# The first mixer's beginning: its modulation as TensorE products, query and key products by channel tile

## The chip, the cores and the metric

The kernel runs on one core of a Trainium2 chip, as one launch. The metric is the device time of one execution in microseconds (us). Five engines work side by side, each with its own queue in program order: TensorE (PE; its weight loads PEld), VectorE (DVE), ScalarE (ACT), GpSimd (POOL) and SyncE (SP), which here issues the loads. They wait for each other by semaphores. Two levels of TensorE's clock appear in the profile, 1.2 and 2.4 GHz; the granted clock is written as a share of the upper one.

## The reference

A sequence of 256 tokens with 1024 channels passes through two blocks of two layers each. What the change touches is the beginning of the first layer of the first block:

```python
c_act = jax.nn.silu(c)
mod = (c_act @ w_ada[l] + b_ada[l])[:, None, :]
sh1, sc1, g1, sh2, sc2, g2 = jnp.split(mod, 6, axis=-1)
h = _rms(x, norm1[l]) * (1.0 + sc1) + sh1
y = _mlstm_mixer(h, a_w_in[j], a_b_if[j], a_h_norm[j], a_w_out[j])
x = x + g1 * y
```

`_mlstm_mixer` projects h to queries and keys (512 columns each), values, output gate (1024 each) and 8 gate columns, mixes the tokens with a gated, chunked recurrence (here as one masked product per head), normalises, multiplies by the sigmoid of the output gate and projects back. A layer of 16 experts follows.

## The kernel before

Activations lie with channels on partitions: 8 channel tiles (KT) of 128 x 256 tokens. A matrix product in 32-bit precision is made of three products: `split` writes a rounded copy of an operand, the high half (ACT, line 371 for weights), and the rest, the low half (DVE, line 374), and `mm3` (lines 381 to 383) forms high x high, high x low and low x high into one sum.

The modulation (`ada`, line 604) has 6 x 8 = 48 columns of 128 channels. For one column a weight tile of 128 x 1024 (512 KB) is multiplied by the condition, which has been copied to all partitions, and summed along each row: on DVE in one instruction (line 623), or, from column 16 on and for every other column, on POOL (line 620) with the sum on ACT (line 621). `first_block` (line 1787) has the columns in a list, `filler`, two at a time. The first 16 (shift and scale of the first norm) are made before anything else by `fill(8)`; the other 32 are taken out of the list as fills between pieces of the mixer: one after every second tile of the query/key products, one in each step of the value products, one after every second tile of the output gate and of the projection.

`pre1` then forms the norm: the squares of x are summed over channels with a constant matrix of ones (`x_squares`, line 466 on PE), `rstd` makes the reciprocal root on DVE (lines 412 to 422), `row` spreads it over the partitions (PE, line 427), and `pre` scales each channel tile (DVE, line 475) and splits it into the halves of u (ACT line 361, DVE line 362).

`mlstm` starts with a chain for the gates (16 products at line 1176, exponential and logarithm on ACT, running maxima on DVE at lines 1211 to 1216, decay tiles at 1231 to 1234). The query and key products (line 1238, `ws_tiles`) go tile by tile of the output: 8 outputs, each over all 8 channel tiles with weights of one 512 KB load, evacuated by ACT (line 1239). The value products (`tokens_by_cols`) go over the channel tiles, two in a step, with four sums in PSUM. Then come the scores (line 1251), the mix, the output gate and the projection.

All loads are issued by SP in program order. Weights of the first mixer pass through a ring of 9 raw slots; a load waits until the slot's last reader is done. The order on each engine comes from a scheduler of the framework, which places the instructions when the program is built. Behind the mixer the same queue issues the expert weights.

The second mixer (`ada_first`, lines 634 to 664) already has 16 modulation columns of another matrix as TensorE products: the condition's 8 channel tiles stand as weights of 32 columns, the weight tile moves, the 8 products of a column fall on four groups of 32 partitions (line 661), a copy brings the 128 x 128 result into SBUF (line 663), and a product with a constant matrix of ones and zeros adds the four groups and turns the row into a column (line 653).

Of the kernel before, what the change touches and what calls it, by code (L numbers as in the profile page):

```python
# [19 lines left out]
KT = 8  # L20
# [141 lines left out]
def lay_out(inp):  # L162
# [17 lines left out]
    v.add("conds", np.stack([vec_cols(g["c_2"][0]), vec_cols(g["c_ctx_2"])], axis=2))  # L180
# [54 lines left out]
class Kernel:  # L235
# [16 lines left out]
    def load_first(self, pool):  # L252
# [4 lines left out]
        nc.sync.dma_start(self.xT, A["xT"])  # L257

    def load_second(self, pool):
        nc, A = self.nc, self.A  # L260
        nc.sync.dma_start(self.consts, A["consts"])
# [208 lines left out]
    def pre(self, pool, u, s, rb, gs, sh):  # L470

        nc = self.nc
        for k in range(KT):
            t = pool.tile([128, S], F32, tag="xs", name="xs", bufs=self.xs_bufs)
            nc.vector.scalar_tensor_tensor(t, self.xs(k, s), gs[:, k:k + 1], rb[:, :S], op0=ALU.mult, op1=ALU.mult)
            self.split_sum(u[:, k, 0], u[:, k, 1], t, sh[:, k:k + 1])
# [157 lines left out]

    def ada_first(self, pool):
# [3 lines left out]
        conds = pool.tile([128, KT, 32], F32, name="cond_cols", bufs=1)  # L639
        nc.gpsimd.memset(conds, 0.0)  # L640
        nc.scalar.activation(conds[:, :, :2], self.v("conds").rearrange("p (k s) -> p k s", s=2), AF.Silu)
# [7 lines left out]
        def some():  # L649
            if last:  # L650
                t, rows = last.pop()
                st = self.st()[:, :2]
                nc.tensor.matmul(st, rows, self.k("sum4")[:, :2], start=True, stop=True)
                nc.vector.tensor_add(self.mod2[0][:, t], st, self.v("b_ada2_0")[:, t:t + 1].to_broadcast([128, 2]))
            if todo:
                ps = self.tp()[:, :128]
                w = ahead.pop(0)
                ahead.extend(islice(raws, 1))
                for k in range(KT):
                    j = 32 * (k % 4)  # L660
                    nc.tensor.matmul(ps[j:j + 32], conds[:, k], w[:, k * 128:k * 128 + 128], start=(k < 4), stop=(k >= 4))
                rows = pool.tile([128, 128], F32, tag="grow", name="grow", bufs=2)
                nc.any.tensor_copy(rows, ps)
                last.append((todo.pop(0), rows))
# [411 lines left out]

    def router(self, wg, mod, g):
# [42 lines left out]
    def tokens_by_cols(self, u, src):  # L1120
# [43 lines left out]
    def mlstm(self, pool, u, gate, router):  # L1164
# [700 lines left out]
```

## Time and profile before

| | us |
|---|---|
| median of 3 runs | 2707.77 (2702.83 to 2710.92) |
| the profiled execution's own time | 2702.24 |
| its span in the profile | 2700.4 |
| first mixer: first weight product on DVE | 9.43 |
| first product of queries and keys on PE | 39.19 |
| last evacuation of queries and keys | 77.81 |
| copies of the values | 98.68 |
| first issue of expert weights into the ring | 152.68 |

A row of the timeline gives start, length, engine, line, what is written and read, shapes, and how many instructions it merges; in brackets the idle time before it and what ended it. A group by line gives busy time, mean of one in ns, and idle time before it. A stretch gives the busy time of every engine in it (with the number of instructions), the granted clock of TensorE, the share of the DMA engines and their rate.

### The profile page before, as it was taken

How to read it: one execution, taken by the hardware profiler on the slowest of the kernel's cores; microseconds unless marked ns; L12 is line 12 of the kernel's file. 1: busy time of each engine (PE TensorE's matmuls, PEld its weight loads, DVE VectorE, ACT ScalarE, POOL GpSimd, SP SyncE). 2: the span in 40 equal slices, each digit the busy share in tenths (PEclk: the TensorE clock that was granted, in tenths of full speed). 3: DMA queues.
4: the chain of work that ended last, by engine and by line, in shares of the span. 5: the costliest groups of instructions: out<-in, count | busy, mean ns of one | idle time of the engine just before them, and what ended most of it. 6: DMA issues, size and time to landing. Idle time of an engine off the chain costs nothing.

```text
span 2700.4 us, 38571 instructions
## 1 busy us (share of the span) xinstructions
PE 2476.7 (92%) x14614; PEld 1915.4 (71%) x14614; DVE 1653.1 (61%) x3421; ACT 935.7 (35%) x1641; POOL 473.4 (18%) x420
## 2 busy tenths in 40 slices
PE   3988997887999899999899999999899999898998
PEld 3874344566444688888775788888788888786997
DVE  7873125786222368656866777673858665958555
ACT  3541103564011232223327542222432223445543
POOL 2330101544000000002406420000400001534100
PEclk9989998888999899999899999999999999999999
DMA  8789997667999356532340236453247443322453
GB/s 320 276 327 410 420 419 261 232 211 298 381 398 419 141 185 221 168 120 88 135 138 1 79 110 209 154 190 91 74 148 226 155 150 97 118 83 94 160 178 123
DMA packets 123305, 540.62 MB, mean 200 GB/s; under 512 B 14688, under 2 KB 14944, under 8 KB 98272
## 3 DMA queue, kind: packets, MB, share of 16 engines
q1 hardware_dynamic: 123104, 538.00, 55.2%
q8 instruction: 119, 1.95, 0.3%
q14 instruction: 82, 0.67, 0.1%
HBM read 536.90 MB, written 1.05 MB: 199 GB/s over the span
## 4 chain that ended last, share of the span: by engine, by line
PE 56%; DVE 7%; issue 1%; ACT 1%; DMA 1%; POOL 0%; DVEq 0%; SPq 0%; ACTq 0%; POOLq 0%
PE mm L382 16%; PE mm L383 16%; PE mm L381 16%; DVE lo L374 2%; PE tp L383 1%; PE tp L382 1%; PE tp L381 1%; PE mm L868 1%; PE tp L860 1%; PE mm L848 1%; DVE ysq L499 1%; DMA raw<-in_w_ada_dram 1%; ACT hi L371 0%; DVE mx L818 0%; DVE rs_x L412 0%
## 5 line engine op out<-in xcount | busy, mean ns | idle before, releaser
L374 DVE TENSOR_TENSOR lo<-raw,hi 128x512 fp32r<-128x512 f32 (+1 forms) x780 | 574.7, 766 | 381.5 <-ACT hi L371 379.1
L371 ACT ACTIVATE hi<-raw 128x1024 fp32r<-128x1024 f32 (+1 forms) x390 | 404.7, 1044 | 872.3 <-PE mm L382 571.4
L381 PE MATMUL mm<-u,hi 128*128 128x512 f32 (+1 forms) x1608 | 572.8, 360 | 17.5 <-ACT hi L371 9.6
L383 PE MATMUL mm<-u,lo 128*128 128x512 f32 (+1 forms) x1608 | 576.8, 360 | 5.2 <-DVE lo L374 5.2
L382 PE MATMUL mm<-u,hi 128*128 128x512 f32 (+1 forms) x1608 | 578.2, 360 | 2.3 <-POOL u L359 1.3
L381 PEld LDWEIGHTS mm<-u,hi 128*128 128x128 f32 x1608 | 306.9, 193 | 64.5 <-ACT hi L371 11.2
L383 PEld LDWEIGHTS mm<-u,lo 128*128 128x128 f32 x1608 | 310.5, 193 | 49.1 <-DVE lo L374 6.9
L382 PEld LDWEIGHTS mm<-u,hi 128*128 128x128 f32 x1608 | 310.6, 193 | 47.3 <-DVE u L362 2.5
L382 PE MATMUL mm<-act,hi 128*128 128x512 f32 (+1 forms) x612 | 223.0, 364 | 0.1
L381 PE MATMUL mm<-act,hi 128*128 128x512 f32 (+1 forms) x612 | 222.3, 363 | 0.0
L383 PE MATMUL mm<-act,lo 128*128 128x512 f32 (+1 forms) x612 | 222.2, 363 | 0.0
L1691 PE MATMUL mm<-raw,xg 128*32 128x512 f32 x1696 | 199.2, 593 | 1.1 <-DMA raw<-in_moe_gu_dram 1.1
L623 DVE SCALAR_TENSOR_TENSOR junk<-raw,conds 128x1024 f32<-128x1024 f32 x128 | 155.6, 1222 | 66.3 <-DMA raw<-in_w_ada_dram 65.9
L620 POOL TENSOR_TENSOR raw<-raw,cond 128x1024 f32<-128x1024 f32 x48 | 119.9, 2502 | 244.7 <-DMA raw<-in_w_ada_dram 224.8
L501 POOL TENSOR_TENSOR acc<-acc,ysq 128x768 f32<-128x768 f32 x45 | 92.5, 2065 | 394.0 <-DVE ysq L499 348.8
L623 DVE SCALAR_TENSOR_TENSOR raw<-raw,conds 128x1024 f32<-128x1024 f32 x128 | 156.6, 1229 | 2.4
L628 POOL TENSOR_TENSOR mod<-mod,vecs 128x16 f32<-128x16 f32 (+1 forms) x28 | 10.3, 366 | 764.7 <-DVE raw L623 721.4
L1691 PEld LDWEIGHTS mm<-raw,xg 128*32 128x32 f32 x1696 | 63.0, 110 | 112.3 <-issue 107.6
L381 PEld LDWEIGHTS mm<-act,hi 128*128 128x128 f32 x612 | 117.5, 192 | 18.7 <-issue 1.2
L382 PEld LDWEIGHTS mm<-act,hi 128*128 128x128 f32 x612 | 117.7, 192 | 18.2 <-DVE act L351 0.7
L383 PEld LDWEIGHTS mm<-act,lo 128*128 128x128 f32 x612 | 117.5, 192 | 17.2
L1723 DVE TENSOR_TENSOR hy<-hy,tp 128x512 f32<-128x512 f32 x56 | 38.2, 686 | 149.3 <-PE tp L1720 149.1
(458 smaller groups left out, 4102.5 us busy)
## 6 DMA issues: line engine op xcount, KB each, us to landing
raw<-in_moe_gu_dram SPq DMA_DIRECT2D x122, 1024.0 KB, 17.8
raw<-in_w_ada_dram SPq DMA_DIRECT2D x200, 512.0 KB, 4.5
raw<-in_ffn_wi_dram SPq DMA_DIRECT2D x176, 512.0 KB, 4.3
raw<-in_moe_down_dram SPq DMA_DIRECT2D x63, 1024.0 KB, 17.8
raw<-in_ffn_wo_dram SPq DMA_DIRECT2D x48, 448.0 KB, 3.9
raw<-in_w_k_dram SPq DMA_DIRECT2D x32, 512.0 KB, 3.9
raw<-in_ffn_wo_dram SPq DMA_DIRECT2D x24, 512.0 KB, 4.2
raw<-in_ffn_wo_last_dram SPq DMA_DIRECT2D x22, 512.0 KB, 4.1
```

Source lines behind the costliest of these rows:

```text
L371: self.mark = self.nc.scalar.activation(hi[:, :m], raw[:, c:c + m], AF.Copy)
L374: self.nc.vector.tensor_sub(lo[:, i:e], raw[:, c + i:c + e], hi[:, i:e])
L381: nc.tensor.matmul(out, lh, rh, start=start, stop=False, skip_group_check=mixed)
L382: nc.tensor.matmul(out, lh, rl, start=False, stop=False, skip_group_check=mixed)
L383: nc.tensor.matmul(out, ll, rh, start=False, stop=stop, skip_group_check=mixed)
L499: nc.vector.scalar_tensor_tensor(t[:, 2], y, self.gate(d, s), kern.xs(d, s), op0=ALU.mult, op1=ALU.mult)
L501: (nc.vector if d == KT - 2 else nc.gpsimd).tensor_add(self.acc[s], self.acc[s], t)
L620: nc.gpsimd.tensor_mul(out, rows, c)
L623: nc.vector.scalar_tensor_tensor(out, rows, 1.0, c, op0=ALU.mult, op1=ALU.mult, accum_out=mod[:, t, s:s + 1])
L848: nc.tensor.matmul(sc[:, :nk], qk[a][half, 512 + t * 128:640 + t * 128], qk[b][half, :nk], start=(i == 0), stop=(i == 2))
L1691: nc.tensor.matmul(ps[t:t + 32], x[:, t:t + 32], w[i][:, s], start=first, stop=last)
L1723: nc.vector.tensor_add(yv, yv, tp)
```

## The change

The 16 columns of the first modulation are made by TensorE as in the second mixer, two per channel tile (shift and scale of that tile), from a new layout of the weights, `w_ada_first`. `first_input` goes over the channel tiles: it makes the columns of the next tile, forms the tile's u, and adds its share to all 8 query/key outputs, which are kept as sums in the four PSUM banks until the end; `a_qk` is laid out by channel tile for it. The outputs are evacuated by ACT and DVE in turn at the start of `mlstm`. The constants are loaded ahead of the condition, the second part of the constants and the gate weights behind all 24 tiles. The fills that stood among the query/key products move into the value products: two per step in place of one. The helpers `cond_cols`, `column` and `column_end` are split out of `ada_first`; the constant they sum with, `sum2`, now lies in the first load.

```diff
-    v.add("conds", np.stack([vec_cols(g["c_2"][0]), vec_cols(g["c_ctx_2"])], axis=2))
+    v.add("conds", np.stack([vec_cols(g["c"][0]), vec_cols(g["c_2"][0]), vec_cols(g["c_ctx_2"])], axis=2))
+    v.add("sum2", (np.arange(128)[:, None] % 32 == np.arange(2)[None, :]).astype(np.float32))
...
+    order = np.arange(2 * KT).reshape(2, KT).T.ravel()
+    A["w_ada_first"] = np.ascontiguousarray(still_tiles(g["w_ada"][0, :, :2048])[order])
...
-    A["a_qk"] = still_tiles(aw[:, :1024])
+    A["a_qk"] = np.ascontiguousarray(ktiles(aw[:, :1024]))
...
         nc.sync.dma_start(self.xT, A["xT"])
+        nc.sync.dma_start(self.consts, A["consts"])
...
+    def column(self, pool, conds, w):
+        nc = self.nc
+        ps = self.tp()[:, :128]
+        for k in range(KT):
+            j = 32 * (k % 4)
+            nc.tensor.matmul(ps[j:j + 32], conds[:, k], w[:, k * 128:k * 128 + 128], start=(k < 4), stop=(k >= 4))
+        rows = pool.tile([128, 128], F32, tag="grow", name="grow", bufs=2)
+        nc.any.tensor_copy(rows, ps)
+        return rows
+
+    def column_end(self, rows, out, bias):
+        nc = self.nc
+        n = out.shape[1]
+        st = self.st()[:, :n]
+        nc.tensor.matmul(st, rows, self.v("sum2")[:, :n], start=True, stop=True)
+        nc.vector.tensor_add(out, st, bias.to_broadcast([128, n]) if n > 1 else bias)
...
+    def first_input(self, pool, p, mod, g):
...
+        banks = [self.mm() for _ in range(4)]
+        out = [banks[m // 2][:, m % 2 * S:m % 2 * S + S] for m in range(8)]
...
+        def columns(k):
+            rows = [(t, self.column(p, conds, self.ring.raw(A["w_ada_first"][2 * k + i:2 * k + i + 1].rearrange("t p k -> p t k"))))
+                    for i, t in enumerate((k, KT + k))]
+            for t, r in rows:
+                self.column_end(r, mod[:, t], bias[:, t:t + 1])
+            nc.vector.scalar_tensor_tensor(gs[:, k:k + 1], mod[:, KT + k], 1.0, g[:, k:k + 1], op0=ALU.add, op1=ALU.mult)
+            return self.chunks(self.ring, A["a_qk"][k:k + 1].rearrange("k p n -> p k n"))
+
+        w = columns(0)
+        rb = p.tile([128, S], F32, name="rb_first", bufs=1)
+        nc.scalar.activation(rb, self.x_rows(pool), AF.Copy)
+        for k in range(KT):
+            self.pre_tile(pool, u, 0, rb, gs, mod[:, :KT, 0], k)
+            now = w
+            if k < KT - 1:
+                w = columns(k + 1)
+            for m in range(8):
+                self.mm3(out[m], *now[m], u[:, k, 0], u[:, k, 1], k == 0 and m % 2 == 0, k == KT - 1, True)
+        return u, out
...
-    def tokens_by_cols(self, u, src):
+    def tokens_by_cols(self, u, src, fills):
...
-            self.fill()
+            self.fill(fills)
...
-    def mlstm(self, pool, u, gate, router):
+    def mlstm(self, pool, u, q_and_k, gate, router):
...
+        qk = t_([128, 8, S], "qk")
+        for m, ps in enumerate(q_and_k):
+            scale = 1.0 if m < 4 else 128.0 ** -0.5
+            if m % 2:
+                nc.vector.tensor_scalar(qk[:, m], ps, scale, None, op0=ALU.mult)
+            else:
+                nc.scalar.activation(qk[:, m], ps, AF.Copy, scale=scale)
...
-        for m, ps in self.ws_tiles(self.ring, A["a_qk"], u, [S] * 8):
-            nc.scalar.activation(qk[:, m], ps[:, :S], AF.Copy, scale=(1.0 if m < 4 else 128.0 ** -0.5))
-            if m % 2:
-                self.fill()
-        acc = self.tokens_by_cols(u, A["a_v"])
+        acc = self.tokens_by_cols(u, A["a_v"], 2)
...
-                    self.filler = ada[0]
-                    self.fill(8)
+                    self.filler = ada[0][8:]
+                    u, q_and_k = self.first_input(pool, p, mod, self.v("norm1_0"))
                     self.load_second(pool)
```

The queue of SP from the second load on, before, up to the first query/key weights:

```order
L257 DMA xT<-in_xT_dram 128x2048
L600 DMA cond_75<-in_conds_dram 128x1024
L326 DMA raw<-in_w_ada_dram 128x1024 x16
L261 DMA consts<-in_consts_dram 128x1154
L262 DMA consts_72<-in_consts_dram 128x1054
L264 DMA rows<-in_rows_dram 128x312
L267 DMA wr<-in_w_router_dram 128x8x16
L1170 DMA g_224<-in_a_g_dram 128x64
L326 DMA raw<-in_a_qk_dram 128x1024 x2
```

and in the changed kernel:

```order
L260 DMA xT<-in_xT_dram 128x2048
L261 DMA consts<-in_consts_dram 128x1154
L605 DMA cond_76<-in_conds_dram 128x1024
L329 DMA raw<-in_w_ada_first_dram 128x1024 x2
L329 DMA raw<-in_a_qk_dram 128x1024
L329 DMA raw<-in_w_ada_first_dram 128x1024 x2
L329 DMA raw<-in_a_qk_dram 128x1024
L329 DMA raw<-in_w_ada_first_dram 128x1024 x2
```

The constants have moved ahead of the first weights; of every three weight tiles two are now of the modulation and one of queries and keys.

TensorE in the middle of the query/key products, before (`a` and `lf` belong to the gate chain):

```order
L381 MATMUL mm<-u,hi 128x256
L382 MATMUL mm<-u,hi 128x256
L383 MATMUL mm<-u,lo 128x256
L381 MATMUL mm<-u,hi 128x256
L382 MATMUL mm<-u,hi 128x256
L427 MATMUL tp<-consts,a 128x128 x8
L383 MATMUL mm<-u,lo 128x256
L381 MATMUL mm<-u,hi 128x256
L382 MATMUL mm<-u,hi 128x256
```

and in the changed kernel, from the first products of the fourth channel tile on (line 384 to 386 is `mm3`, 654 a column of the next tile, 664 its sum):

```order
L384 MATMUL mm<-u,hi 128x256 x2
L664 MATMUL st<-vecs,grow 128x1
L385 MATMUL mm<-u,hi 128x256
L386 MATMUL mm<-u,lo 128x256
L384 MATMUL mm<-u,hi 128x256
L385 MATMUL mm<-u,hi 128x256
L654 MATMUL tp<-raw,cond_cols 32x128 x8
L386 MATMUL mm<-u,lo 128x256
L385 MATMUL mm<-u,hi 128x256
L386 MATMUL mm<-u,lo 128x256
L384 MATMUL mm<-u,hi 128x256
L664 MATMUL st<-vecs,grow 128x1
```

Columns and sums of the next channel tile now stand between the products; the gate chain is no longer there.

VectorE in the last steps of the value products and the beginning of the scores, before (623 is a fill, `lo` a low half of value weights, `v` the copy of the values):

```order
L623 SCALAR_TENSOR_TENSOR raw,mod_0_78<-raw,cond_75 128x1024
L374 TENSOR_TENSOR lo<-raw,hi 128x512 x4
L623 SCALAR_TENSOR_TENSOR raw,mod_0_78<-raw,cond_75 128x1024
L374 TENSOR_TENSOR lo<-raw,hi 128x512 x4
L623 SCALAR_TENSOR_TENSOR raw,mod_0_78<-raw,cond_75 128x1024
L1245 COPY v<-mm 128x512 x2
L374 TENSOR_TENSOR lo<-raw,hi 128x512
```

and in the changed kernel (628 is a fill, 1307 the decay times the scores):

```order
L628 SCALAR_TENSOR_TENSOR raw,mod_0_79<-raw,cond_76 128x1024 x2
L377 TENSOR_TENSOR lo<-raw,hi 128x512 x4
L628 SCALAR_TENSOR_TENSOR raw,mod_0_79<-raw,cond_76 128x1024 x2
L377 TENSOR_TENSOR lo<-raw,hi 128x512 x4
L1300 COPY v<-mm 128x512
L628 SCALAR_TENSOR_TENSOR raw,mod_0_79<-raw,cond_76 128x1024
L1307 TENSOR_TENSOR dt_784<-dt_784,mm 128x256
L1307 TENSOR_TENSOR dt_785<-dt_785,mm 128x128
L1307 TENSOR_TENSOR dt_784<-dt_784,mm 128x256
L628 SCALAR_TENSOR_TENSOR raw,mod_0_79<-raw,cond_76 128x1024
```

Each step now has two fills on VectorE, and two more stand behind the copy of the values, one of them among the scores.

## Rows read from the trace of the kernel before

**Rows 1.** The page, part 1: busy time of each engine, share, instructions.

```profile
PE 2476.7 (92%) x14614; PEld 1915.4 (71%) x14614; DVE 1653.1 (61%) x3421; ACT 935.7 (35%) x1641; POOL 473.4 (18%) x420
```

**Rows 2.** Stretches: length, busy of PE, PEld, DVE, ACT, POOL, PEclk, DMA share, GB/s.

```profile
20.00:30.00 10.00, 0.00 (x0) 0.00 (x0) 9.80 (x18) 0.00 (x0) 1.22 (x2) 1.00 1.03 410
...
60.00:70.00 10.00, 10.00 (x83) 10.00 (x82) 8.58 (x32) 5.80 (x10) 1.27 (x1) 0.94 0.68 253
...
90.00:100.00 10.00, 10.00 (x45) 8.00 (x44) 8.80 (x12) 4.01 (x6) 4.84 (x3) 1.00 0.97 367
...
250.00:300.00 50.00, 43.84 (x315) 23.06 (x313) 16.74 (x32) 8.57 (x16) 9.63 (x5) 0.93 1.02 421
```

**Rows 3.** Timeline of SP, the issue of loads, 152 to 202 us.

```profile
152.68 15.39 SPq L326 DMA_DIRECT2D raw<-in_moe_gu_dram  x8
...
200.38 20.51 SPq L326 DMA_DIRECT2D raw<-in_moe_gu_dram  x12
```

**Rows 4.** Timeline of the beginning: start, length, engine, line, idle before, releaser.

```profile
9.43 1.23 DVE L623 SCALAR_TENSOR_TENSOR raw<-raw,cond 128x1024 f32<-128x1024 f32 x1 [9.43 <-ACT sq L459]
...
28.59 1.22 DVE L623 SCALAR_TENSOR_TENSOR raw<-raw,cond 128x1024 f32<-128x1024 f32 x1
...
30.05 3.54 PE L466 MATMUL st<-consts,sq 128*128 128x1 f32 x16 [30.05 <-DMA consts<-in_consts_dram]
...
35.43 0.69 PE L427 MATMUL tp<-consts,rs_y 128*128 128x128 f32 x2 [1.83 <-DVE rs_y L422]
...
39.19 0.58 PE L381 MATMUL mm<-u,hi 128*128 128x256 f32 x1 [3.07 <-ACT hi L371]
...
44.77 3.33 PE L1176 MATMUL st<-u,gw 128*16 128x256 f32 x16 [1.42 <-DVE gw L351]
...
47.93 0.28 PE L383 MATMUL mm<-u,lo 128*128 128x256 f32 x1
```

**Rows 5.** Second mixer: two timeline rows, then groups of instructions by line.

```profile
451.74 1.08 PE L661 MATMUL tp<-raw,cond_cols 128*32 128x128 f32 x16
...
496.41 1.08 PE L661 MATMUL tp<-raw,cond_cols 128*32 128x128 f32 x32
...
L653 PE MATMUL st<-consts,grow 128*128 128x2 f32 x30 | 4.9, 239 | 4.0 <-DVE grow L663 2.1 <-DVE mod L654 1.9
...
L663 ACT COPY grow<-tp 128x128 f32<-128x128 f32 x5 | 1.2, 260 | 5.0 <-PE tp L661 5.0
```

**Rows 6.** Groups by line, first 170 us: busy, mean ns, idle before, releasers.

```profile
L475 DVE SCALAR_TENSOR_TENSOR xs<-xT,gs,tp 128x256 f32<-128x256 f32 x8 | 3.4, 471 | 0.8 <-PE tp L427 0.8
...
L361 ACT ACTIVATE u<-xs,mod 128x256 fp32r<-128x256 f32 x8 | 3.6, 498 | 25.6 <-DVE xs L475 25.5
...
L620 POOL TENSOR_TENSOR raw<-raw,cond 128x1024 f32<-128x1024 f32 x16 | 40.8, 2547 | 53.2 <-DMA raw<-in_w_ada_dram 36.1 <-ACT hi L371 7.2 <-DVE lo L374 6.3
```

**Rows 7.** Timeline of ACT and DVE, then two groups of the first 170 us.

```profile
77.81 0.36 ACT L1239 ACTIVATE qk<-mm 128x256 f32<-128x256 f32 x1
...
82.35 2.49 DVE L374 TENSOR_TENSOR lo<-raw,hi 128x512 fp32r<-128x512 f32 x4
...
98.68 1.39 DVE L1245 COPY v<-mm 128x512 f32<-128x512 f32 x2 [1.19 <-PE mm L1134]
...
L374 DVE TENSOR_TENSOR lo<-raw,hi 128x512 fp32r<-128x512 f32 x64 | 54.4, 887 | 2.3 <-ACT hi L371 2.3
L623 DVE SCALAR_TENSOR_TENSOR raw<-raw,cond 128x1024 f32<-128x1024 f32 x32 | 42.4, 1350 | 9.4 <-ACT sq L459 9.4
```

**Rows 8.** Timeline of the gate chain: DVE and one ACT row.

```profile
51.61 1.28 ACT L1186 ACT_TABLE_LOAD   x1
...
59.70 0.42 DVE L1211 TENSOR_TENSOR am<-tp,consts 128x256 f32<-128x256 f32 x1 [0.94 <-PE tp L427]
...
67.42 0.42 DVE L1231 TENSOR_TENSOR dt<-tp,consts 128x256 f32<-128x256 f32 x1 [0.73 <-PE tp L427]
```

**Rows 9.** Stretch 57.9 to 61.3 us, columns as in rows 2.

```profile
57.90:61.30 3.40, 3.40 (x18) 3.40 (x17) 2.43 (x10) 0.91 (x1) 2.36 (x1) 0.50 0.84 318
```

More of the change, by code (lines that the diff above doesn't have):

```diff
@@ L257, in load_first @@
         nc.sync.dma_start(self.xT, A["xT"])
+        nc.sync.dma_start(self.consts, A["consts"])
     def load_second(self, pool):
         nc, A = self.nc, self.A
-        nc.sync.dma_start(self.consts, A["consts"])
         nc.sync.dma_start(self.consts1, A["consts1"])
@@ L470, in pre, with pre_tile @@
     def pre(self, pool, u, s, rb, gs, sh):
-        nc = self.nc
         for k in range(KT):
-            t = pool.tile([128, S], F32, tag="xs", name="xs", bufs=self.xs_bufs)
-            nc.vector.scalar_tensor_tensor(t, self.xs(k, s), gs[:, k:k + 1], rb[:, :S], op0=ALU.mult, op1=ALU.mult)
-            self.split_sum(u[:, k, 0], u[:, k, 1], t, sh[:, k:k + 1])
+            self.pre_tile(pool, u, s, rb, gs, sh, k)
+    def pre_tile(self, pool, u, s, rb, gs, sh, k):
+        t = pool.tile([128, S], F32, tag="xs", name="xs", bufs=self.xs_bufs)
+        self.nc.vector.scalar_tensor_tensor(t, self.xs(k, s), gs[:, k:k + 1], rb[:, :S], op0=ALU.mult, op1=ALU.mult)
+        self.split_sum(u[:, k, 0], u[:, k, 1], t, sh[:, k:k + 1])
     class Output:
@@ L651, in some @@
                 t, rows = last.pop()
-                st = self.st()[:, :2]
-                nc.tensor.matmul(st, rows, self.k("sum4")[:, :2], start=True, stop=True)
-                nc.vector.tensor_add(self.mod2[0][:, t], st, self.v("b_ada2_0")[:, t:t + 1].to_broadcast([128, 2]))
+                self.column_end(rows, self.mod2[0][:, t], self.v("b_ada2_0")[:, t:t + 1])
             if todo:
-                ps = self.tp()[:, :128]
                 w = ahead.pop(0)
                 ahead.extend(islice(raws, 1))
[L659 to L664, printed above, removed]
+                last.append((todo.pop(0), self.column(pool, conds, w)))
         self.next_first = some
@@ L1075, in pre1 @@
         return u
+    def first_input(self, pool, p, mod, g):
+        nc, A = self.nc, self.A
+        conds = self.cond_cols(p, 0, 1)
+        gs = p.tile([128, KT], F32, name="gs_first", bufs=1)
+        u = pool.tile([128, KT, 2, S], F32R, tag="u", name="u", bufs=1)
+        banks = [self.mm() for _ in range(4)]
+        out = [banks[m // 2][:, m % 2 * S:m % 2 * S + S] for m in range(8)]
+        bias = self.v("b_ada_0")
+        def columns(k):
[16 more added lines that the diff above has]
+        return u, out
     def router(self, wg, mod, g):
@@ L1811, in first_block @@
                     self.ada_first(p)
-                u = self.pre1(pool, mod, self.v(f"norm1_{l}"))
+                    u = self.pre1(pool, mod, self.v(f"norm1_{l}"))
                 router = lambda: self.router(wg, mod, self.v(f"norm2_{l}"))
                 if l == 0:
-                    self.mlstm(p, u, mod[:, 16:24], router)
+                    self.mlstm(p, u, q_and_k, mod[:, 16:24], router)
                     self.fill(len(self.filler))
```

11 lines of the change are left out of this document (7 added, 4 removed).

## The prediction

> **What bounds the kernel now.** I read the page first, then the stretches of the first 300 us, the timeline of the first mixer engine by engine, and last the prices of single operations, some of which the first mixer does not have yet and the second one does. The page names TensorE: busy 92% of the span [rows 1]. The stretches show that this is no single limit [rows 2]. From 20 to 30 us TensorE does nothing, VectorE is busy 9.80 of 10 us, the DMA engines are full (1.03). From 60 to 70 and from 90 to 100 us TensorE is full, and VectorE has 8.58 and 8.80 of 10. From 250 us, in the experts, the DMA engines set the pace (1.02, 421 GB/s). So this change is worth what it does to the end of the first mixer. From there the time passes on one for one: the queue starts on expert weights at 152.7 us behind the mixer's last tiles, and the next group is issued at 200.4 us, when the first experts free their slots [rows 3]. Both move with the mixer.
>
> The timeline of the beginning shows why TensorE is late [rows 4]. VectorE multiplies 16 weight tiles by the condition, from 9.43 to 29.8 us. The sums of squares wait until 30.05 us for a constant loaded behind those tiles. The row statistics end at 35.4 us. The first products start at 39.19 us, but halt until 47.9 us, because VectorE still owes the low halves. From there TensorE is nearly dense to the value copies at 98.68 us. What the reader is to see: VectorE's 19 us are at the front, and TensorE's real start is 47.9.
>
> **The change, part by part.** All sums are made against the profiled execution, 2702.24 us (span 2700.4 and 1.84 around it). The median of the three runs is 5.5 us above it.
>
> *First loads.* The constants go ahead of the condition. At the 410 GB/s of this stretch [rows 2] their 128 x 1154 fp32 numbers (591 kB) cost 1.45 us, so the first weight tile, in use at 9.43 us before [rows 4], is there at about 10.5.
>
> *Columns on TensorE.* 16 products of 1.22 us leave VectorE (19.5 us) [rows 4]. The second mixer shows the price on TensorE [rows 5]: one column is 16 records in 1.08 us at the half clock, two are 32 records in 1.08 us at full clock, the drain of the last included, so 0.4 us each. Each also needs a copy (0.26 us on ScalarE) and a summing product (two records of 0.24 us). These are the very operations, so no bound is needed.
>
> *Start-up.* In order on TensorE: column, copy, sum, column, copy, sum (4 us, to 14.5), sums of squares 3.54 us (to 18), statistics on VectorE 1.8 us (TensorE's wait for them) plus the two low halves that the order puts among them, 1.2 us (to 21), broadcast 0.69, its copy 0.4, scaling 0.47, high half 0.50 [rows 4, 6]: the first query/key product starts at about 24 us. Those 24 products begin at the half clock: the 16 gate products at 44.77 us took 3.33 us, 0.208 each, 256 columns at 1.2 GHz, after waits of 1.5 to 3 us; later 83 records fill 10 us [rows 2, 4], 0.117 each. I take 4.5 us, so 28.5.
>
> *Seven further channel tiles.* Each is 24 products (2.8 us), two columns (0.8), two sums (0.5): 4.1 us of TensorE. The order puts each sum a few products behind its column, and the column's drain (its last record lasts some 0.3 of the 1.08 us), the copy (0.26) and two hand-overs, 0.8 us by my estimate, are longer than those products (0.5 us): I add 0.3 per column, so 4.7. The floor is 4.1; the DMA engines would need 3 x 512 KB, 3.8 us, and do not bind. The other end is the chain from the last sum of a tile to the next tile's first product, two additions and the gain (0.2 each), scaling 0.47, high half 0.50, hand-overs 0.3, against 1.4 us of products left to cover it: 5.2. So 28.5 + 7 x 4.7 = 61.4, and 0.6 for fill multiplications on GpSimd that now run in here: 62 us (57 to 67). Before, the last query/key tile was evacuated at 77.81 us [rows 7]. This stage gains 16 us.
>
> *What has moved behind it.* Before, the gate chain and four fills ran beside the query/key products; now they stand behind, and the four steps of the value products carry two fills each. VectorE's list from 62 us to the value copies: 16 low halves (2.49 us per four [rows 7]) 10.0; six fills x 1.22 = 7.3, the other two standing behind the first copy; the gate chain: reductions 59.70 to 63.37 = 3.7, decay tiles 67.42 to 70.4 = 3.0, some 14 small ops of 0.16 = 2.2, and a wait of 2 us for ScalarE's two table loads of 1.28 us with an exponential between them [rows 8], 10.9 in all; four evacuations of 0.42, 1.7. Then GpSimd. Undisturbed, a low half takes 0.62 us and a fill 1.22; over the whole mixer their means are 0.887 and 1.350 [rows 7]. The excess, 64 x 0.265 + 32 x 0.13 = 21 us, I lay on GpSimd's 16 multiplications of 2.55 us [rows 6], during which an operation of VectorE can stand still: 1.3 each on these two lines, 1.65 with the others that are hit; none if the coincidence is by chance, 2.55 if every one blocks. Five fall into this stretch: 5 x 1.65 = 8.2 (0 to 12.7). Sum 38.1, and 0.9 for the last products: the copies start at 101 us against 98.68: +2.3 us. TensorE alone needs less: 96 products at 45 per 10 us [rows 2] are 21.3 us, gates 5.
>
> *Scores.* Two fills now stand among the score products, 2.4 us of VectorE; one falls into a wait, I take 1.5.
>
> *Everything else.* Output gate and projection keep their fills and order. Loads total the same. The second mixer's column code only reads another constant: nothing. Evacuations on two engines: counted.
>
> Sum: -15.8 at the query/key stage, +19.6 given back by what had been hidden beside it: **+3.8 us**, 2706 on the profiled execution, **2712 on the median**. I expect that the gain of the first 50 us is spent by 105 us.
>
> **The rivals.** *One, faster: TensorE sets the pace of the value stage.* If the first multiplications of GpSimd fall into the query/key stage and the gate chain's waits swallow low halves, VectorE's 38 us shrink to TensorE's 21.3 + 5 + 1.7 = 28. With a stage of 57 to 60 us the copies come at 86 to 88: -11 and 1.5 back, about -10 to -12; 2697. For it: VectorE will have slack of about 1.5 us in each channel tile. Against it: before, with half the fills in this stage, VectorE was already busy 8.80 of 10 us [rows 2].
>
> *Two, slower: TensorE stays at the half clock in the channel-tile loop.* A column, a wait for its copy, a few products, a wait for the row: from 57.9 to 61.3 us the granted clock was 0.50, 1.2 GHz [rows 9], after TensorE had waited in the gate chain. At 1.2 GHz a tile costs 24 x 0.208 + 2 x 0.8 + 0.5 + 0.6 = 7.7 instead of 4.7. Seven tiles are +21, with some of it hidden under fills: 2727 to 2732; it decides from three tiles on (9 us). Against it: no wait in the loop should reach 1 us, and the full stretches of before, with gaps that short, ran at 0.94 to 1.00 [rows 2]. The Trainium skill (TensorE: Matmul & The Clock Gate, HAM oscillation) speaks against this loop shape: with channel tiles outermost and a wait between short bursts, the clock drops at every tile, and it advises to do all channel tiles of an output before waiting, which is the order before. By that rule the time would be this rival's; the trace agrees that waits bring the half clock [rows 9], and has no loop of this shape to show.
>
> *Three, slower: ScalarE comes late in the value stage.* Its queue is in order, and behind each of GpSimd's multiplications stands an accumulation. With two per step the high halves of the last value tiles stand behind two of them. If GpSimd's pair (2 x 2.55 us) is not done, that is up to 5 us, at two steps: +5 to +10 on top, 2717 to 2722. For it: GpSimd's row counts 36.1 us of waiting for fills to land [rows 6].
>
> **How the numbers follow.** A measurement here can tell some 0.3%, 8.1 us, from no change. Forecast (-4 to +9 us around the median): 0.47, of it 0.42 within 8.1 us and 0.05 above. Rival one 0.23: 0.21 faster, 0.02 within. Two 0.10, all slower. Three 0.20: 0.19 slower, 0.01 within. Rounded: faster 0.22, same 0.44, slower 0.34. The range runs from rival one's far end, 2695, over rival three, to the lower half of rival two, 2728; the likeliest case alone is 2704 to 2717.
>
> **What would show it.** Right: first query/key product near 24 us, low halves of the last channel tile near 60, periods of 4.5 to 5.2 us, VectorE above 9 of 10 us from 62 to 100, value copies at 98 to 104, first expert weights issued at 150 to 160. Wrong: value copies before 92 us (rival one); a granted clock of 0.50 over several channel tiles (rival two); high halves in the value stage waiting for GpSimd (rival three). If the channel-tile period is above 6 us at the full clock, my term for hand-overs is wrong.

## The result, and the profile after

The changed kernel takes **2725.62 us** (median of 5 runs, 2722.16 to 2732.47) where the kernel before took 2702.83 beside it (5 runs, 2697.65 to 2710.92): 1.0085 of its time, 95% interval 1.0067 to 1.0104, some 23 us. The forecast was 2712; the time lies inside the range, above the likeliest case's 2704 to 2717. As a difference the forecast was +3.8 us, and +23 (18 to 28) were measured. The profiled execution has a span of 2723.8 us, 23.4 more than before.

The page's first part, to be held against [rows 1]:

```profile
PE 2510.5 (92%) x14902; PEld 1926.6 (71%) x14902; DVE 1642.9 (60%) x3414; ACT 938.3 (34%) x1655; POOL 476.0 (17%) x419
```

VectorE has 10 us less to do, and TensorE is busy 34 us longer. The columns and their sums are about 16 us of that (7.5 and 4.1 us for twelve of them between 28 and 58 us). So TensorE also takes longer for the work that it had before.

The beginning, on the timeline (columns as in [rows 4]):

```profile
10.95 1.08 PE L654 MATMUL tp<-raw,cond_cols 128*32 128x128 f32 x16 [10.95 <-DMA raw<-in_w_ada_first_dram]
...
24.30 0.76 PE L384 MATMUL mm<-u,hi 128*128 128x256 f32 x2
...
52.09 0.48 DVE L480 SCALAR_TENSOR_TENSOR xs<-xT,gs_first,rb_first 128x256 f32<-128x256 f32 x1
...
55.54 4.78 POOL L625 TENSOR_TENSOR raw<-raw,cond 128x1024 f32<-128x1024 f32 x2 [47.12 <-DMA raw<-in_w_ada_dram]
...
57.98 2.63 DVE L480 SCALAR_TENSOR_TENSOR xs<-xT,gs_first,rb_first 128x256 f32<-128x256 f32 x1
...
61.20 0.74 PE L384 MATMUL mm<-u,hi 128*128 128x256 f32 x4 [2.61 <-ACT u L364]
...
68.44 0.41 DVE L1225 TENSOR_SCALAR qk<-mm 128x256 f32<-128x256 f32 x1
...
87.62 5.14 POOL L625 TENSOR_TENSOR raw<-raw,cond 128x1024 f32<-128x1024 f32 x2
87.86 8.85 DVE L377 TENSOR_TENSOR lo<-raw,hi 128x512 fp32r<-128x512 f32 x4 [0.55 <-ACT hi L374]
...
103.55 0.68 DVE L1300 COPY v<-mm 128x512 f32<-128x512 f32 x1
...
125.56 0.42 DVE L1332 TENSOR_TENSOR qk<-rb,mm 128x256 f32<-128x256 f32 x1 [1.10 <-PE mm L1331]
```

The first query/key product stands at 24.30 us in place of 39.19 [rows 4]. The last query/key sum is evacuated at 68.4 instead of 77.81 [rows 7], so 9 us are won. The copies of the values start at 103.55 instead of 98.68 [rows 7]: the 9 us are gone, and 5 more (5.6 by the first copy of all, which ScalarE made at 97.97 before). Two places show where. At 57.98 us the scaling of the last channel tile takes 2.63 us, beside a pair of GpSimd multiplications; the tile before took 0.48. TensorE waits 2.61 us for it, and then runs at a granted clock of 0.83 in the mean from 60 to 70 us. At 87.86 us four low halves take 8.85 us, beside the next pair; four took 2.49 [rows 7].

The change itself probably opened the scaling to this. It reads the spread root from SBUF now (`rb_first`), where it read PSUM (`tp` [rows 6]). In the first mixer of both traces the VectorE operations that read PSUM and began while GpSimd multiplied a fill were not lengthened (11 before, 13 after); of those that read two tiles or more in SBUF, 11 of 13 before and 13 of 15 after were. A version that keeps the row in PSUM was not run.

Three stretches (columns as in [rows 2]):

```profile
30.00:40.00 10.00, 9.99 (x123) 8.48 (x121) 4.98 (x14) 2.94 (x7) 0.00 (x0) 1.00 0.88 305
...
60.00:70.00 10.00, 8.48 (x48) 7.27 (x49) 6.54 (x13) 5.64 (x12) 2.72 (x2) 0.83 0.17 64
...
90.00:100.00 10.00, 7.85 (x24) 5.83 (x25) 10.00 (x10) 5.35 (x8) 5.49 (x2) 0.67 0.56 189
```

In the channel-tile loop TensorE is full at a granted clock of 1.00 (2.4 GHz), and VectorE stands idle for half of the time. From 90 to 100 us VectorE is full and TensorE waits. So one stage has the slack and the next the overload.

SP's issues of expert weights, against [rows 3]:

```profile
164.07 8.45 SPq L329 DMA_DIRECT2D raw<-in_moe_gu_dram  x8
...
207.87 0.97 SPq L329 DMA_DIRECT2D raw<-in_moe_gu_dram  x2
```

The first is 11.4 us later than before, the next group 7.5 us. So the mixer accounts for about 8 of the 23 us. Going on through the trace, issue by issue: the delay is 7.9 us at the end of the first experts, 11.2 at 890 us, where the second block's weights begin to be loaded, 17.1 at 1290, 21.7 at 2020 and 24 from 2280 on. Two of these issues, before and then after:

```profile
398.41 8.64 SPq L326 DMA_DIRECT2D raw<-in_moe_down_dram  x4
...
2605.69 0.33 SPq L326 DMA_DIRECT2D raw<-in_ffn_wo_last_dram  x1
```

```profile
406.35 8.93 SPq L329 DMA_DIRECT2D raw<-in_moe_down_dram  x4
...
2629.73 0.33 SPq L329 DMA_DIRECT2D raw<-in_ffn_wo_last_dram  x1
```

The delay grows slowly through a second block in which the change alters no instruction. That growth shows in this group by line, one stretch of 100 us in the second block, the same work in both kernels; first before, then after:

```profile
L383 PE MATMUL mm<-u,lo 128*128 128x512 f32 x84 | 32.7, 389 | 0.0
...
L381 PE MATMUL mm<-act,hi 128*128 128x512 f32 x64 | 24.9, 389 | 0.0
```

```profile
L386 PE MATMUL mm<-u,lo 128*128 128x512 f32 x82 | 32.4, 396 | 0.0
...
L384 PE MATMUL mm<-act,hi 128*128 128x512 f32 x64 | 24.9, 389 | 0.0
```

The same products with u take 396 ns in place of 389, those with act 389 as before; some 600 us later it is the products with act that take 396. Their starts tell it more exactly: before, all but some 1% of the products of 512 columns with u, act or o in the second block start 226 or 227 ns apart; after, those of some tiles 231 to 235 (mean 233.3). About 2220 are slow, and 2220 x 6.6 ns = 14.6 us. The 3.3 us that are lost between the first experts and 890 us are not explained by this. They fall into the second mixer, where single executions scatter: experiment 1 makes up 3.3 us in the same stretch.

### The profile page after: what moved, and what is told of

Its sections match the earlier page's. It is cut to its first block, busy times and chain, and to the rows that moved or that the text cites. A ratio compares the mean times of both kernels' runs of the same rounds, so it can differ in the third digit from the quotient of the medians.

```text
span 2723.8 us, 39177 instructions
## 1 busy us (share of the span) xinstructions
PE 2510.5 (92%) x14902; PEld 1926.6 (71%) x14902; DVE 1642.9 (60%) x3414; ACT 938.3 (34%) x1655; POOL 476.0 (17%) x419
## 3 DMA queue, kind: packets, MB, share of 16 engines
HBM read 536.90 MB, written 1.05 MB: 197 GB/s over the span
## 4 chain that ended last, share of the span: by engine, by line
PE 58%; DVE 6%; ACT 1%; issue 1%; POOL 0%; DVEq 0%; ACTq 0%; POOLq 0%
PE mm L385 16%; PE mm L384 16%; PE mm L386 16%; PE tp L384 1%; PE tp L386 1%; PE tp L385 1%; PE mm L890 1%; DVE lo L377 1%; PE tp L882 1%; PE mm L870 1%; DVE ysq L504 1%; PE mm L956 1%; PE mm L957 1%; PE mm L955 0%; ACT hi L374 0%
```

## The experiments

**Theory Placement** says: the change makes the row of small vectors (`vecs`) 40 bytes longer (eight floats of `c`, two of `sum2`); every tile behind it in a partition moves by 32 bytes, and with it the second block's; that is the growth behind 1000 us. **Theory Beginning** says: everything comes from the first mixer and what starts late behind it. Each ratio below is against runs of the kernel before that were made beside it, with its 95% interval.

**1. Eight more floats, on the changed kernel.** All later tiles move by another 32 bytes.

```diff
     v.add("sum2", (np.arange(128)[:, None] % 32 == np.arange(2)[None, :]).astype(np.float32))
+    v.add("pad", np.zeros((128, 8), np.float32))
```

> The changed kernel with eight more (unused) floats in the row of small vectors, so that every tile behind it begins 32 bytes further on than in the changed kernel. Theory Placement: of the 23 us that the change costs, some 15 are lost behind the first mixer, because the 40 bytes that the change adds to this row move the second block's inputs u and act by 32 bytes, and products of 512 columns then start 231 to 235 ns apart where they started 227 ns apart before; with the 32 bytes more they start 227 ns apart again, and the time is 2708 to 2713 us. Theory Beginning: all 23 us come from the first mixer and from what starts late behind it; moving tiles does nothing: 2722 to 2730 us.

Measured: 2716.03 us, 1.0058 (1.0039 to 1.0078). Neither. The products with u still took 394 ns in the stretch at 1010 us, so the spacing explains only 1 us of the 9.6 by which the median lies under the changed kernel's; the intervals of the two overlap, and the rest stays open. Pulling the tiles another 32 bytes along did not mend the second block.

**2. Ten more floats, on the kernel before.** The row gets the changed kernel's length, the tiles behind it move by the same 32 bytes, and nothing else is changed.

> The kernel before, with ten more (unused) floats in the row of small vectors, so that this row has the length that it has in the changed kernel; the program is otherwise the one before. Placement: 512-column products of the second block start 231 to 235 ns apart in about half of the cases, as after the change, and the time is 2714 to 2721 us (12 to 18 us over the kernel before). Beginning: no difference, 2698 to 2708 us.

Measured: 2713.70 us, 1.0051 (1.0031 to 1.0072), or +13.8 us (10.2 by the medians). The same stretch as above, in this kernel:

```profile
L383 PE MATMUL mm<-u,hi 128*128 128x512 f32 x82 | 32.4, 396 | 0.0
...
L383 PE MATMUL mm<-act,hi 128*128 128x512 f32 x64 | 24.9, 389 | 0.0
```

Forty unused bytes make the kernel before slower in the same products as the change does. This shows Placement. Up to 1000 us the run is as before (within 1 us at most issues); the loss comes behind it. By the issues it is 9.6 us from 890 to 2617 us, less than its slow products add up to, so a part of their time is hidden or made good elsewhere; where is not known.

**3. The first mixer's fills on VectorE alone**, on experiment 1.

```diff
-                        lambda t, l=l: t >= 16 or t % 2 == 0 if l else (t >= 16 and t % 2 == 0)) for l in range(2)]
+                        lambda t, l=l: bool(l) and (t >= 16 or t % 2 == 0)) for l in range(2)]
```

> The first experiment, and the filling tiles of the first mixer all multiplied and summed on VectorE in one instruction each; none on GpSimd with ScalarE. Theory Collision: VectorE operations of two SBUF inputs that run beside a GpSimd multiplication take 2 to 3 us in place of 0.7 to 1.2; without those the mixer ends 4 to 8 us earlier than in the first experiment, although VectorE has 8 more tiles of 1.23 us. Theory Load: VectorE has too much to do in the value stage, whoever slows it; 8 tiles more make the mixer 5 to 10 us later.

Measured: 2706.06 us, 1.0015 (1.0003 to 1.0028), 10 us under experiment 1. Collision, and by more than it said: the value copies come at 99.4 instead of 107.0, and the experts' issue near 200 us is 3.4 us *earlier* than before the change, where experiment 1 had it 11.2 later.

**4. Four fills in the channel-tile loop**, one behind each second tile, one per value step; on experiment 1.

```diff
             for m in range(8):
                 self.mm3(out[m], *now[m], u[:, k, 0], u[:, k, 1], k == 0 and m % 2 == 0, k == KT - 1, True)
+            if k % 2:
+                self.fill()
...
-        acc = self.tokens_by_cols(u, A["a_v"], 2)
+        acc = self.tokens_by_cols(u, A["a_v"], 1)
```

> The first experiment, with one filling step in each value step (as before the change) and four in the channel-tile loop of the query and key products, one behind each second tile, where VectorE stands idle for half of the time. Theory Load: the value copies come 5 us earlier or more (at 98 us or below), and the time is 4 to 8 us below the first experiment. Rival Bandwidth: the loop's weights already take 0.86 of the DMA engines; the fills' 4 MB delay the loop by 8 us or more, which eats the gain: within 3 us of the first experiment, or slower.

Measured: 2726.13 us, 1.0086 (1.0066 to 1.0106): 10 us over experiment 1. The low half of the last channel tile comes at 74.4 instead of 63.7. The rival's outcome; what makes the loop longer is taken up in experiment 11.

**5. 27 more floats**, on the changed kernel: 128 bytes on from before.

> The changed kernel with 27 more (unused) floats in the row of small vectors: every tile behind it begins 128 bytes further on than in the kernel before, where 8 floats gave 64 bytes, and there the products of 512 columns whose input is the left-hand u or act still started 233 to 234 ns apart. Theory Placement, with a period of 128 bytes: all of them start 227 ns apart again, and 10 to 14 us of what the change costs are gone: 2706 to 2713 us, with the experts of the first block still 7 to 11 us later than before. Rival: the period is another, or it is how tiles lie to one another: half of the products stay at 231 to 235 ns, 2716 to 2726 us.

Measured: 2721.72 us, 1.0069 (1.0043 to 1.0095). The rival. The slow products now start 229 to 238 ns apart. Sorted by the tile that each product reads, as the program lays them out, the slow ones are the same in the changed kernel and in experiments 1, 2 and 5: those whose u, act or o lies in a pool on the right-hand side of memory, which does not move, while their weights lie on the left, which moved by 32, 64 or 128 bytes. Products with both on the left stay at 226.8 ns throughout. So it is the distance between the two that counts, at the four distances that were run.

**6. The same with the fills on VectorE alone.**

> The one before, and the first mixer's filling tiles on VectorE alone. If placement and the collisions of GpSimd with VectorE are separate costs, both gains are had: 2693 to 2699 us, some 7 us below the kernel before, and experts that start 3 us earlier than before. If they overlap (the same microseconds of TensorE), 2700 to 2706 us.

Measured: 2713.24 us, 1.0030 (1.0014 to 1.0047), 8.5 us under experiment 5. Above both expected ranges, since experiment 5, on which it stands, did not mend the placement; the gain of the fills is there once more.

**7. The kernel before with the first mixer's fills on VectorE alone**, the edit of experiment 3.

> The kernel before with its first mixer's filling tiles on VectorE alone, nothing else. Theory Collision: the kernel before pays for the collisions too (12 of its 16 GpSimd multiplications fell beside a VectorE operation of two SBUF inputs), and gains 4 to 12 us as the changed kernel did: 2692 to 2699 us; then the change itself gives nothing beside the same fills. Rival: only the changed kernel gains, because it alone has two fills in a value step; before, VectorE is the bound of the beginning (8.84 of 10 us busy) and 16 tiles more of 1.23 us make it 2704 to 2715 us.

Measured: 2688.66 us, 0.9952 (0.9932 to 0.9973). Collision: the kernel before had been paying too, and this version beats both kernels. VectorE's groups over the first mixer, in experiment 7:

```profile
L623 DVE SCALAR_TENSOR_TENSOR raw<-raw,cond 128x1024 f32<-128x1024 f32 x48 | 57.6, 1226 | 9.4 <-DMA raw<-in_w_ada_dram 9.3
L374 DVE TENSOR_TENSOR lo<-raw,hi 128x512 fp32r<-128x512 f32 x64 | 42.4, 701 | 2.2 <-ACT hi L371 2.1
```

Against [rows 7], 16 more fills cost 15.2 us, and the 64 low halves take 42.4 us in place of 54.4. With the other operations that are no longer held up, VectorE comes out ahead: it is busy 132.5 us up to the end of the mixer at 159, where it was 142.0 up to 170. GpSimd's 40.8 us [rows 6] and ScalarE's 16 sums are gone.

**8. One fill per value step, the four others at the output gate**, on experiment 5.

```diff
             if m % 2:
-                self.fill()
+                self.fill(2)
...
-        acc = self.tokens_by_cols(u, A["a_v"], 2)
+        acc = self.tokens_by_cols(u, A["a_v"], 1)
```

> The changed kernel with 27 more floats, and one filling step in each value step, as before the change; the four others go to the output-gate products, two steps behind each second tile in place of one. Theory Load: the value copies come 4 us earlier or more than with two steps (99 us or below), the output gate ends at the same time or later, and the time is 0 to 5 us below that of the changed kernel with 27 floats. Rival: the value stage waits for something else (TensorE's products, the loads), and nothing changes at the value copies.

Measured: 2724.27 us, 1.0078 (1.0056 to 1.0101), the same as experiment 5 within the intervals. The last value copy comes at 101.8 instead of 110.3 (not at the 99 that Load named) and the last mixed tile at 120.0 instead of 127.9, but the experts' issue near 200 us is 7.2 us late against 7.8. Load is right about the value stage, but what is taken from there is paid at the output gate: VectorE is busy 33.65 of the 35 us from 125 to 160.

**9. The ten floats in a tile of their own**, in the first block's pool, so that the second block's tiles lie where they lay before the change.

```diff
-    v.add("conds", np.stack([vec_cols(g["c"][0]), vec_cols(g["c_2"][0]), vec_cols(g["c_ctx_2"])], axis=2))
-    v.add("sum2", (np.arange(128)[:, None] % 32 == np.arange(2)[None, :]).astype(np.float32))
+    v.add("conds", np.stack([vec_cols(g["c_2"][0]), vec_cols(g["c_ctx_2"])], axis=2))
...
+        self.firsts = pool.tile([128, 10], F32, name="firsts")
+        nc.sync.dma_start(self.firsts, A["firsts"])
         nc.sync.dma_start(self.vecs, A["vecs"])
...
```

> The changed kernel with its ten new floats in a small tile of the first block alone, loaded by a DMA of its own, so that the row of small vectors is as long as before the change and every tile of the second block begins where it did before. In the runs so far, products were slow (229 to 238 ns) exactly where their input lay in a pool on the right-hand side, which does not move, and their weights in one on the left, which had moved by 32, 64 or 128 bytes; where both had moved, or neither, they stayed at 227 ns. Theory Distance: with the old distance between the two they are all at 227 ns again, 12 to 14 us are gone, and what is left is the beginning alone: 2708 to 2714 us. Rival: something else of the change slows the second block: 2718 to 2726 us.

Measured: 2712.09 us, 1.0032 (1.0020 to 1.0044), or +8.6 us (5.4 to 11.9). The stretch of the second block:

```profile
L387 PE MATMUL mm<-u,hi 128*128 128x512 f32 x84 | 32.7, 389 | 0.0
...
L386 PE MATMUL mm<-act,hi 128*128 128x512 f32 x64 | 24.9, 389 | 0.0
```

All at 389 again, x84 as before, and all but some 1% of the starts 226 or 227 ns apart. Distance is shown: 1.0085 - 1.0032 is 14.3 us for the placement (12.6 by the medians), near the 14.6 of the slow products. What is left, 8.6 us, is the beginning, with a load of its own in front (first query/key product at 24.97 us, not 24.30). Single executions differ there: in this trace the first 24 query/key products take 5.4 us, where the changed kernel's take 3.6, and the experts' issue near 200 us is 12.3 us late, not 7.5.

**10. The same with the first mixer's fills on VectorE alone.**

> The one before, and the first mixer's filling tiles on VectorE alone. Theory Distance: 12 to 14 us below the changed kernel with 27 floats and the same fills: 2697 to 2702 us. Against the kernel before with these fills (2688.7 us) the change itself then costs 8 to 13 us. Rival: it costs nothing any more (within 3 us of 2688.7).

Measured: 2693.78 us, 0.9971 (0.9958 to 0.9983), 18 us under experiment 9. One group of each over the first mixer, experiment 9 and then 10:

```profile
L379 DVE TENSOR_TENSOR lo<-raw,hi 128x512 fp32r<-128x512 f32 x60 | 61.9, 1068 | 3.3 <-ACT hi L376 3.3
```

```profile
L379 DVE TENSOR_TENSOR lo<-raw,hi 128x512 fp32r<-128x512 f32 x60 | 39.5, 697 | 3.7 <-ACT hi L376 3.6
```

The changed kernel is faster than the kernel before once its two hidden costs are taken out, but not faster than that kernel with the same fills (experiment 7). The interval of that one, 0.9932 to 0.9973, overlaps this one's, so that the change itself costs something there (5 us by the ratios) is likely and not shown.

**11. Experiment 10 with four of the fills in the loop**, the edit of experiment 4.

> The one before, with one filling step in each value step and four in the channel-tile loop. With the GpSimd multiplications in the loop these four cost it 11 us (its last tile at 74.4 in place of 63.7). Theory Collision: that was the slowed work of VectorE on the input tiles; with fills on VectorE alone, which is idle for half of the loop, the loop is at most 4 us longer, the value copies come 5 us earlier than without, and the time is 3 to 8 us below the one before. Rival: the loads of the fills delay the loop, or any instruction put ahead of VectorE's work on the next input tile does; the loop is 8 us or more longer, and nothing is gained.

Measured: 2706.22 us, 1.0014 (1.0000 to 1.0028). The rival again; the loop ends 12 us later (73.1 against 60.9) with no GpSimd in it. VectorE's timeline there:

```profile
48.49 1.22 DVE L630 SCALAR_TENSOR_TENSOR raw<-raw,cond 128x1024 f32<-128x1024 f32 x1
...
49.63 1.22 DVE L630 SCALAR_TENSOR_TENSOR raw<-raw,cond 128x1024 f32<-128x1024 f32 x1
...
50.78 0.48 DVE L367 SCALAR_TENSOR_TENSOR u<-xs,mod,u 128x256 fp32r<-128x256 f32 x1
52.21 0.16 DVE L668 TENSOR_TENSOR mod<-st,vecs 128x1 f32<-128x1 f32 x1 [0.95 <-PE st L667]
55.75 0.16 DVE L668 TENSOR_TENSOR mod<-st,vecs 128x1 f32<-128x1 f32 x1 [3.38 <-PE st L667]
```

The fill stands between the low halves of the weights and that of u, for which TensorE waits; and the next tile's sum comes 3.38 us late, where the wait was 1.82 in the tile before. That tile takes 9.3 us instead of 5.4. VectorE's idle half is made of waits of 1 to 2 us in a chain, and there is no room for 2.4 us in any of them. The fills' loads also go ahead of the next tile's in the queue; how much of the 3.9 us is theirs was not tried apart.

**12. The kernel before with the fills of both mixers on VectorE alone.**

```diff
-                        lambda t, l=l: t >= 16 or t % 2 == 0 if l else (t >= 16 and t % 2 == 0)) for l in range(2)]
+                        lambda t: False) for l in range(2)]
```

> The kernel before with the filling tiles of both mixers on VectorE alone (in the seventh experiment only those of the first). In the second mixer, between 440 and 600 us, 24 GpSimd multiplications of 2.51 us stand beside VectorE, where the low parts of the weights take 1042 ns on average (48 of them) for 0.68 alone. Theory Collision: what held in the first mixer holds there too, and 4 to 10 us more are gained than with the first mixer's fills alone: 2679 to 2685 us. Rival: 24 tiles more at 1.23 us on VectorE (30 us) are as dear there as the collisions, of which 48 x 0.36 = 17 us show in the low parts: 2686 to 2696 us.

Measured: **2649.41 us**, 0.9806 (0.9788 to 0.9825), some 53 us below the kernel before and 39 below experiment 7. That is far beyond what Collision said. The second mixer with its projection, from its first weights to the next issue of experts, is 237.4 us long before and 197.5 now (columns as in [rows 2]); first before, with three of VectorE's groups in that stretch and two moments in it, then experiment 12:

```profile
444.00:681.40 237.40, 192.09 (x1128) 147.79 (x1132) 186.20 (x437) 125.11 (x258) 102.54 (x76) 0.83 0.66 246
...
L374 DVE TENSOR_TENSOR lo<-raw,hi 128x512 fp32r<-128x512 f32 x64 | 61.8, 1001 | 0.3 <-issue 0.3
...
L412 DVE TENSOR_SCALAR rs_x<-ss 128x16 f32<-128x16 f32 x4 | 5.0, 1238 | 0.1
...
459.06 2.86 POOL L620 TENSOR_TENSOR raw<-raw,cond 128x1024 f32<-128x1024 f32 x1 [14.37 <-DMA raw<-in_w_ada_dram]
459.58 2.37 DVE L1324 SCALAR_TENSOR_TENSOR ang<-turns,ang 128x16 f32<-128x16 f32 x1
```

```profile
429.00:626.50 197.50, 176.16 (x1128) 138.75 (x1132) 161.96 (x486) 96.08 (x212) 28.31 (x45) 0.88 0.80 298
...
L374 DVE TENSOR_TENSOR lo<-raw,hi 128x512 fp32r<-128x512 f32 x64 | 43.4, 701 | 1.3 <-ACT hi L371 1.3
L623 DVE SCALAR_TENSOR_TENSOR raw<-raw,cond 128x1024 f32<-128x1024 f32 x24 | 29.0, 1219 | 0.4 <-DMA raw<-in_w_ada_dram 0.4
...
L412 DVE TENSOR_SCALAR rs_x<-ss 128x16 f32<-128x16 f32 x4 | 1.0, 258 | 0.0
```

VectorE does 32 fills more (38.8 us, 24 of them in the row shown) and is busy 24 us *less*; TensorE's idle time in the stretch falls from 45.3 to 21.3 us, and its granted clock rises from 0.83 to 0.88. An operation on 16 elements per partition took 2.37 us at 459.58, beside a GpSimd multiplication that had begun half a microsecond earlier; the 16-element groups fall from 1238 to 258 ns. I had priced the low halves alone (17 us); small operations, those of the row statistics among them, were hit for 1 to 2 us each. To count them: in the stretch before, 36 of VectorE's operations last 54.1 us longer than the fastest tenth of the same operation, each beside a GpSimd operation; in experiment 12 it is 3.3 us. So the collisions are gone. Two more things go with them. ScalarE loses its 32 sums of 1.05 us, and the loads no longer wait for those sums to free a slot: SyncE waited 29.5 us for them before, and 9.8 us for VectorE's in their place now. How the 40 us fall to the three was not taken apart. This is the best version that was run; it beats both kernels. The changed kernel with all fills on VectorE and its floats in a tile of their own was not tried.

## Why the prediction was right or wrong

*Start-up: right.* First column at 10.95 us (said about 10.5; its two terms, 9.43 and 1.45, add to 10.9), sums of squares at 14.84 (14.5), first query/key product at 24.30 (24; the terms listed add to 23.1).

*Channel tiles: the sum right, and a stall that it had at next to nothing.* From the first product of one tile to that of the next it is 4.8, 3.8 and 4.2 us, then 5.3 to 5.4, where I took 4.7 throughout and had 5.2 as the far end. Over the loop the short ones make up for the long ones. Without the stall it would have ended at about 62.2 us (an estimate: the seventh tile's start at 53.18, one more period of 5.38, and 3.67 for the last 24 products as in experiment 10), which is the 62 of the forecast. The term that failed is "0.6 for fill multiplications on GpSimd that now run in here": one pair of them held the last tile's scaling (0.48 to 2.63 us), TensorE waited 2.61 us and came back at a lower clock, and the last 24 products took 5.2 us. The last product ended at 66.4. The last evacuation, at 68.4, stood behind one more low half that was held by GpSimd (1.44 us). Of the 16 us to gain, 9 were there.

*Value stage: the place and the sum about right.* From the last product on it took 37.1 us where 39.0 were summed, so the copies came at 103.55 (said 101, 98 to 104). VectorE was not full throughout, as the sign "VectorE above 9 of 10 us from 62 to 100" had it: it was busy 12.6 of the 18 us to 80, and 22.7 of the 23.5 from there to the copies. "Five fall into this stretch: 5 x 1.65 = 8.2" was the right mechanism: five low halves lasted 9.3 us longer in it than alone. The total was right too, 16 x 1.65 = 26.4 us: in the trace of before, 17 operations of VectorE in the first 170 us last 26.8 us longer than the fastest tenth of the same operation, each beside a GpSimd operation; in experiment 7 it is 1.8 us. Its parts were not. The 0.62 us of a low half is the spacing inside a merged row, and one alone lasts 0.69 us, so the two lines have some 17 us and not 21, and other operations have the rest. Whether it was chance was left open ("none if the coincidence is by chance"). Experiments 3, 6, 7 and 10 settle it: without GpSimd's multiplications the low half falls to about 0.70 us, and 8 to 18 us are gained. The Trainium skill (SBUF — State Buffer, Who interferes with whom) says it outright: VectorE with two SBUF inputs contends with a GpSimd instruction that reads SBUF, and the later one blocks until the first is done. The 2.37 us of the 16-element operation agree: it ended with the multiplication, at 461.9 us. The operation of line 412 reads one tile of SBUF and was held as well, which that sentence does not cover.

*Scores: 1.5 said, 3.3 measured* (8.2 us late at the last mixed tile, less 4.9 at the copies; 2.6 if the copies are counted from ScalarE's first). The last mixed tile before, against 125.56 after:

```profile
117.39 0.42 DVE L1277 TENSOR_TENSOR qk<-rb,mm 128x256 f32<-128x256 f32 x1 [1.13 <-PE mm L1276]
```

A further GpSimd multiplication at 119.78 us stands beside a low half of 2.83 us between the mixed tiles.

*The sum of the beginning: +3.8 said, +8.6 measured (5.4 to 11.9)*, by experiment 9, where the second block lies as before. The sign and the cause hold ("the gain of the first 50 us is spent by 105 us"); the size was off by the loop's end and the scores, and by the extra load of experiment 9. The first issue of expert weights, at 164.07 us, missed its sign (150 to 160).

*"Everything else": this is the step that failed.* It has "Loads total the same" and "only reads another constant: nothing". It has no term for the row of small vectors, which grows by 40 bytes and moves the tiles behind it, and none for anything behind the second mixer. There these bytes cost some 14 us, more than the whole beginning (experiments 2 and 9). No rival had it. That the time lies in the range all the same is luck: the range was drawn from -13 to +20 us around a median of 2707.77, its upper part stood for rival two, and +23 were measured from a median of 2702.83.

*Rival one* (value stage at TensorE's pace, copies before 92 us) did not come; only the kernel before without GpSimd's fills comes near (92.2, experiment 7). *Rival two* named a time of 2727 to 2732, near the measured one, for a reason that the trace refutes: the granted clock was 1.00 from 30 to 60 us. The Trainium skill's rule on loops over channel tiles (TensorE: Matmul & The Clock Gate, HAM oscillation) speaks of a loop in which each tile waits for its data; here TensorE's single waits inside the loop were 0.3 us or less from 28 to 58 us, and the clock fell only behind the 2.61 us wait of the last tile. *Rival three* (ScalarE late) came in a small part: ScalarE waited 1.25 and 1.61 us for GpSimd's products at 90.0 and 92.8 us, and the next high halves stood behind those sums, until 93.85. Nothing was lost by it, since VectorE was itself held by GpSimd until 96.7; its low halves had waited 0.55 us for ScalarE at 87.86.

## What to carry to other kernels

Shortening one stage gained nothing here, because what had been hidden in it fell to an engine that is full in the next. Ask what that engine can do in the time won, and whether its waits leave pieces long enough. Before any restructuring, compare the mean of an operation in the crowded stretch with its price alone. Where the two differ beside GpSimd (here 887 to 1068 ns against 700), try first to take the GpSimd work away, though the other engine then has more to do: that won more here than the restructuring. And a change that lengthens a long-lived tile moves all the tiles behind it: compare the mean time of the same products far behind the change before explaining a difference by the change itself.

## What the runs showed of the hardware that was not expected

The time of a TensorE product depended on the distance between its moving input and its weights in memory: at one distance products of 512 columns start 226.7 ns apart, at distances 32, 64 and 128 bytes from it about 233 ns on average, with patterns of their own (231, 232 and 235; 233, 234 and 236; 229 and 238). Which distances are good in general, and by what mechanism, these runs don't tell; a shift by 256 bytes was not tried, for lack of room. And a VectorE operation of 16 elements per partition can last as long as a GpSimd multiplication of 1024 (2.4 us).
